# Seven products of quarters for eight in part of the last matrix product

## The chip, the core and the metric

The kernel runs on one core of a Trainium2 chip. The metric is the device time of one execution in microseconds (us). Three runs of the kernel before took 991.89 to 992.03 us, with a median of 991.94. Engines are named as in the profile: PE is TensorE (matmuls; PEld is its loading of stationary operands), DVE is VectorE, ACT is ScalarE, POOL is GpSimd and SP is SyncE, which here only issues the loads.

## The reference

The reference is a decoder trunk of two layers over 256 tokens of 1024 channels in float32. Each layer is a half-weighted gated feed-forward step, an attention step, and a second feed-forward step; at the end there is an RMS norm. The change lies in the last feed-forward step and the last norm:

```python
def swiglu(h, w_gate, w_up, w_down):
    return (jax.nn.silu(h @ w_gate) * (h @ w_up)) @ w_down
...
        h = h + FFN_RESIDUAL_WEIGHT * swiglu(rmsnorm(h, ffn2_norm[layer]),
                                             ffn2_w_gate[layer], ffn2_w_up[layer], ffn2_w_down[layer])
...
    return rmsnorm(h, final_norm)
```

The inner width of the feed-forward step is 2816, that is 22 blocks of 128. The last product is therefore (256 x 2816) times (2816 x 1024).

## The kernel before, in words

**Numbers in two parts.** Each float32 operand x is kept as a high part in the matmul's rounded float32 format (written by ACT as a copy) and a low part (written by DVE as x minus the high part). A product of two such operands is three matmuls: high by high, high by low, low by high (`product`, L179 to L186, where the three lines L182, L184 and L186 are these three). Weights come from memory as raw tiles of 1 MB, 4 of which fit (`rawp`), and are split into pieces of 1024 columns, high parts (`wh`) by ACT and low parts (`wl`) by DVE, for each of which there are 8 slots (`wp`). Four raw tiles and eight pieces are two units of gate and up weights each.

**Up to the last step** the residual stream `hT` is kept with channels on partitions. Four gate/up stages, three down products and two attention mixers run one after the other, each fed in the same way.

**The gate/up stage** (`ffn_blocks`, L340) of the last step goes over 11 pairs of blocks f, f + 1. For each pair SP loads 1 MB of gate and 1 MB of up weights. For each block TensorE does 8 matmuls of 512 columns for gate, 8 for up (L193), then 8 of 256 each for the low weights (L196). `close` turns the two accumulators into the block: ACT copies one half (L336), DVE adds the other (L337), multiplies the gate by the norm's row (L352), ACT applies SiLU (L353), POOL multiplies the up half by the row (L355), DVE multiplies both (L356), and ACT and DVE split the result (L94, L90). The block is held as 128 inner channels by 256 tokens, high and low, until the last product has used it.

**Turning the stream** (L688 to L694): between the gate/up stage and the last product, TensorE transposes `hT` in 16 pieces of 128 x 128 into four PSUM tiles (L693), and ACT copies them to `h`, now with tokens on partitions: two token tiles t of 128 rows, two column halves c of 512.

**The last product** (`down_last`, L408): the blocks are the stationary operand and the weights the moving one. It has four accumulators, one for each (t, c). For each of the first 18 blocks there are 12 matmuls of 512 columns: 2 t, 2 c, 3 matmuls each. The last four blocks are held back, so that the four accumulators end one after the other; each is then added to `h` by DVE (L432, L439), squared and summed (L711, L707), multiplied by the gains (L715), and after each token tile scaled by the reciprocal root (L728, L729) and stored. Of the last quarter the second half goes to an accumulator of its own, so that the last of this work is small.

**What sets the order.** Every engine works through its own instruction list in order. The lists come from the program's order of calls and a scheduler that moves an instruction ahead where its inputs allow it; tiles are handed out in rotation, and who gets a tile waits for the last reader of the one before.

Of the kernel before, what the change touches and what calls it, by code (L numbers as in the profile page):

```python
# [25 lines left out]
NG = H // HG  # L26
ROT = 16
HALF = ROT // 2
LEAD = 4
EPS = 1e-6  # L30
SCALE = DH ** -0.5
# [31 lines left out]
def trunk(ctx: ExitStack, tc: tile.TileContext, a: dict, out: bass.AP):  # L63
    nc = tc.nc
    PS = bass.MemoryType.PSUM
    const = ctx.enter_context(tc.tile_pool(name="const", bufs=1))
    rawp = ctx.enter_context(tc.tile_pool(name="rawp", bufs=4))
    wp = ctx.enter_context(tc.tile_pool(name="wp", bufs=8))
    xp = ctx.enter_context(tc.tile_pool(name="xp", bufs=1))
# [7 lines left out]
    def atile(shape, dt=F32, name="a"):  # L77
        return ap_.tile(shape, dt, tag="a", name=name)

    def acc(name):  # L80
        return accp.tile([P, 512], F32, tag="acc", name=name)

    def flat(ap):
        return ap.rearrange("p c n -> p (c n)")

    def parts_of(hi, lo, src, scale=1.0, later=None):

        def rest():
            if isinstance(scale, float):
                nc.vector.tensor_sub(lo, src, hi.bitcast(F32))  # L90
# [3 lines left out]
        nc.scalar.activation(hi, src, AF.Copy, scale=scale)  # L94
        (later or (lambda call: call()))(rest)
# [80 lines left out]
    def rows(w, k0, k, c0, n):  # L176
        return w[k0 * P:(k0 + k) * P, c0:c0 + n].rearrange("(k p) n -> p k n", p=P)

    def product(accs, xh, xl, ws, first, last):  # L179

        for ac, (wh, wl) in zip(accs, ws):
            nc.tensor.matmul(ac, xh, wh, start=first, stop=False)  # L182
        for ac, (wh, wl) in zip(accs, ws):
            nc.tensor.matmul(ac, xh, wl, start=False, stop=False)  # L184
        for ac, (wh, wl) in zip(accs, ws):
            nc.tensor.matmul(ac, xl, wh, start=False, stop=last)  # L186
# [94 lines left out]
    class Pieces:  # L281
# [55 lines left out]
        nc.vector.tensor_add(s, ac[:, :S], s)  # L337
        return s

    def ffn_blocks(name, wg, wu, norm, first=None, beside=()):  # L340

        blocks = []

        def both(f, pair):
            acs = [acc(f"{name}_{n}{f}") for n in "gu"]
            cols = slice(f % 2 * P, (f % 2 + 1) * P)
            products_t(acs, [[(wh[:, cols], wl[:, cols]) for wh, wl in w] for w in pair], norm.x, True, True)
            return acs

        def close(f, gate, up):  # L350
            g = joined(gate, f"{name}_g{f}")
            nc.vector.tensor_mul(g, g, norm.row)  # L352
            nc.scalar.activation(g, g, AF.Silu)  # L353
            u = joined(up, f"{name}_u{f}")
            nc.gpsimd.tensor_tensor(u, u, norm.row, op=ALU.mult)  # L355
            nc.vector.tensor_mul(g, g, u)  # L356
# [48 lines left out]
        down_t(name, wd, blocks, after)  # L405


    def down_last(name, w, nk, blocks, h, weight, part, after, tail=4):  # L408


        accs = [[acc(f"dn_{name}_{t}_{c}") for c in range(2)] for t in range(NT)]
        held = []

        def cut(ws, cols):
            return tuple(w[:, cols] for w in ws)

        halves = [slice(c * 512, (c + 1) * 512) for c in range(2)]
        for u in range(nk // 2):
            for i, ws in enumerate(unit(f"{name}_{u}", 2, D, [(None, rows(w, 2 * u, 2, 0, D))])):
                k = 2 * u + i  # L420
                if k < nk - tail:
                    for t in range(NT):
                        product(accs[t], *blocks[t][k], [cut(ws, half) for half in halves], k == 0, False)
                else:
                    held.append((k, ws))
        for t in range(NT):
            for c, half in enumerate(halves):
                n = 512 if (t, c) != (1, 1) else S
                for k, ws in held:
                    product([accs[t][c][:, :n]], *blocks[t][k], [cut(ws, slice(half.start, half.start + n))], False,  # L430
                            k == nk - 1)
                nc.vector.scalar_tensor_tensor(h[t][c], accs[t][c], weight, h[t][c], op0=ALU.mult, op1=ALU.add)  # L432
                part(t, slice(half.start, half.start + n))
            if t:
                end = acc(f"dn_{name}_end")[:, :S]
                for k, ws in held:
                    product([end], *blocks[t][k], [cut(ws, slice(D - S, D))], k == nk - tail, k == nk - 1)
                hc = h[1][1][:, S:]
                nc.vector.scalar_tensor_tensor(hc, end, weight, hc, op0=ALU.mult, op1=ALU.add)  # L439
                part(t, slice(D - S, D), True)  # L440
            after(t)

    def out_t(name, pieces, base, blocks, norm, tail=3):
# [242 lines left out]
    blocks = ffn_blocks("f21", a["ffn2_w_gate"][1], a["ffn2_w_up"][1], n6)  # L686

    h = [[xp.tile([P, 512], F32, tag=f"kx{2 * t + c}", name=f"h_{t}_{c}") for c in range(2)] for t in range(NT)]  # L688
    for t in range(NT):
        for c in range(2):  # L690
            tr = trt(f"h_{t}_{c}")
            for k in range(4):
                nc.tensor.transpose(tr[:, k * P:(k + 1) * P], hT[:, 4 * c + k, t * P:(t + 1) * P], ident)  # L693
            nc.scalar.activation(h[t][c], tr, AF.Copy)  # L694

    parts = [[], []]
    outs = [[None, None] for t in range(NT)]
# [26 lines left out]
    def finish(t):  # L724
# [8 lines left out]
    down_last("f21_d", a["ffn2_w_down"][1], KF,  # L733
              [[tuple(x[:, i, t * P:(t + 1) * P] for i in range(2)) for x in blocks] for t in range(NT)],
              h, 0.5, finish_part, finish)


_INS = ["ffn1_w_gate", "ffn1_w_up", "ffn1_w_down", "ffn2_w_gate", "ffn2_w_up", "ffn2_w_down",
# [23 lines left out]
```

## Time and profile before

| | us |
|---|---|
| median of the three runs | 991.94 |
| the profiled execution | 992.04 |
| its span, first to last instruction | 990.2 |
| last gate/up pair (f = 20, 21) on TensorE | 11.13 (911.20 to 922.33) |
| the 16 transposes | 1.82 (922.33 to 924.15) |
| first 18 blocks of the last product | 49.07 (923.90 to 972.97) |
| held blocks | 11.19 (972.97 to 984.16) |
| rest, to the end of the span | 6.0 |

Times inside the span are counted from its start. Matmuls overlap: one of 512 columns is shown with about 0.39 us, and the next starts after 0.23. A row of the timeline gives the start, the length, the engine, the line, the operation with the tiles it writes and reads, a count where several are merged, and in brackets how long the engine was idle before it and who ended that.

### The profile page before, as it was taken

The numbers are of one execution on the slowest core, as the hardware profiler recorded it, in microseconds if no ns is written. First come the engines' busy times: TensorE is split into PE (matmuls) and PEld (weight loads), VectorE is DVE, ScalarE is ACT, GpSimd is POOL, SyncE is SP. The second block draws the span as 40 slices with busy tenths as digits, with TensorE's granted clock in tenths as the row PEclk, the third lists the DMA queues.
The fourth block names the chain that finished last, engine by engine and source line by source line (L and its number), as shares of the span: only waits on it lengthen the run. The fifth ranks groups of instructions, "written<-read, shape, count | busy, mean of one in ns | idle before, by whom it ended". The sixth has DMA issues, their size and how long they took to land. (4 is left out here: it accounts for less than half of the span.)

```text
span 990.2 us, 15709 instructions
## 1 busy us (share of the span) xinstructions
PE 978.1 (99%) x5892; PEld 863.5 (87%) x5892; DVE 731.2 (74%) x1283; ACT 588.6 (59%) x1079; POOL 164.4 (17%) x194
## 2 busy tenths in 40 slices
PE   8999999999999999999999999999999999999997
PEld 5888888888899888888888888888889998888886
DVE  6987866667787788776678877666687878788642
ACT  7656654467776656655456566545677656665531
POOL 3211111122302211111121111111222022111000
PEclk9999999999999999999999999999999999999999
DMA  9776465653434565555645664666533345655611
GB/s 300 252 253 210 162 213 181 212 173 139 156 121 141 166 197 191 196 193 182 201 161 187 197 204 158 203 201 213 170 129 128 119 142 175 205 175 202 205 57 43
DMA packets 158573, 176.06 MB, mean 178 GB/s; under 512 B 3616, under 2 KB 152608, under 8 KB 158496
## 3 DMA queue, kind: packets, MB, share of 16 engines
q1 hardware_dynamic: 157776, 174.24, 53.6%
q8 instruction: 46, 0.75, 0.3%
q10 hardware_dynamic: 720, 0.82, 0.2%
q14 instruction: 31, 0.25, 0.1%
HBM read 173.99 MB, written 1.05 MB: 177 GB/s over the span
## 5 line engine op out<-in xcount | busy, mean ns | idle before, releaser
L193 PE MATMUL f_g<-x_n,wh_f_g 128*128 128x512 f32 x688 | 180.1, 394 | 0.0
L193 PE MATMUL f_u<-x_n,wh_f_u 128*128 128x512 f32 x688 | 177.3, 390 | 0.0
L193 PEld LDWEIGHTS f_u<-x_n,wh_f_u 128*128 128x128 f32 x688 | 129.1, 188 | 27.3
L193 PEld LDWEIGHTS f_g<-x_n,wh_f_g 128*128 128x128 f32 x688 | 124.1, 189 | 22.6
L355 POOL TENSOR_TENSOR j_f_u<-j_f_u,r_n 128x256 f32<-128x256 f32 x88 | 76.6, 872 | 378.9 <-DVE j_f_u L337 356.6
L193 PE MATMUL dn_f<-act_f,wh_f 128*128 128x512 f32 x528 | 126.5, 391 | 0.0
L157 DVE TENSOR_TENSOR wl_f_u<-raw_f_u,wh_f_u 128x1024 fp32r<-128x1024 f32 x86 | 120.4, 1401 | 1.8 <-ACT wh_f_u L156 1.7
L157 DVE TENSOR_TENSOR wl_f_g<-raw_f_g,wh_f_g 128x1024 fp32r<-128x1024 f32 x86 | 103.5, 1234 | 16.7 <-PE f_g L196 10.6
L193 PEld LDWEIGHTS dn_f<-act_f,wh_f 128*128 128x128 f32 x528 | 96.9, 188 | 18.6
L157 DVE TENSOR_TENSOR wl_f<-raw_f,wh_f 128x1024 fp32r<-128x1024 f32 x72 | 81.9, 1154 | 35.8 <-ACT wh_f L156 26.7
L196 PE MATMUL f_u<-x_n,wl_f_u 128*128 128x256 f32 x688 | 103.3, 283 | 0.0
L196 PE MATMUL f_g<-x_n,wl_f_g 128*128 128x256 f32 x688 | 102.9, 282 | 0.0
L196 PEld LDWEIGHTS f_g<-x_n,wl_f_g 128*128 128x128 f32 x688 | 96.5, 190 | 6.3
L156 ACT ACTIVATE wh_f_g<-raw_f_g 128x1024 fp32r<-128x1024 f32 x86 | 89.4, 1049 | 13.3 <-issue 6.0
L156 ACT ACTIVATE wh_f<-raw_f 128x1024 fp32r<-128x1024 f32 x72 | 67.3, 978 | 49.5 <-PE dn_f L193 27.2
L156 ACT ACTIVATE wh_f_u<-raw_f_u 128x1024 fp32r<-128x1024 f32 x86 | 86.6, 1046 | 15.2 <-PE f_g L193 10.9
L196 PEld LDWEIGHTS f_u<-x_n,wl_f_u 128*128 128x128 f32 x688 | 91.6, 192 | 0.0
L230 POOL TENSOR_TENSOR ss_n<-ss_n,sq_n 128x256 f32<-128x256 f32 x42 | 42.2, 1005 | 248.7 <-ACT sq_n L229 247.8
L94 ACT ACTIVATE act_f<-j_f_g 128x256 fp32r<-128x256 f32 x88 | 36.5, 417 | 72.0 <-DVE j_f_g L356 71.8
L353 ACT ACTIVATE j_f_g<-j_f_g 128x256 f32<-128x256 f32 x88 | 36.8, 418 | 66.6 <-DVE j_f_g L352 66.2
L196 PEld LDWEIGHTS dn_f<-act_f,wl_f 128*128 128x128 f32 x528 | 68.1, 191 | 2.8
L196 PE MATMUL dn_f<-act_f,wl_f 128*128 128x256 f32 x528 | 69.0, 283 | 0.0
(220 smaller groups left out, 1790.6 us busy)
## 6 DMA issues: line engine op xcount, KB each, us to landing
raw_f_g<-in_ffn_w_gate_dram SPq DMA_DIRECT2D x43, 1024.0 KB, 5.2
raw_f_u<-in_ffn_w_up_dram SPq DMA_DIRECT2D x43, 1024.0 KB, 5.2
raw_f<-in_ffn_w_down_dram SPq DMA_DIRECT2D x24, 1024.0 KB, 5.2
raw_f_d<-in_ffn_w_down_dram SPq DMA_DIRECT2D x11, 1024.0 KB, 4.8
raw_f<-in_ffn_w_down_dram SPq DMA_DIRECT2D x12, 768.0 KB, 4.6
raw_qka<-in_a_w_qkv_dram SPq DMA_DIRECT2D x16, 512.0 KB, 4.4
raw_kvb<-in_kv_w_dram SPq DMA_DIRECT2D x12, 512.0 KB, 4.2
raw_va<-in_a_w_qkv_dram SPq DMA_DIRECT2D x4, 1024.0 KB, 5.0
```

The costliest lines, as they stand in the source:

```text
L94: nc.scalar.activation(hi, src, AF.Copy, scale=scale)
L156: nc.scalar.activation(wh, r, AF.Copy)
L157: nc.vector.tensor_sub(wl, r, wh.bitcast(F32))
L193: nc.tensor.matmul(ac, wh, flat(x), start=first and i == 0, stop=False)
L196: nc.tensor.matmul(ac[:, :S], wl, x[:, 0, :], start=False, stop=last and i == len(ws) - 1)
L230: nc.gpsimd.tensor_tensor(self.ss, self.ss, sq, op=ALU.add)
L353: nc.scalar.activation(g, g, AF.Silu)
L355: nc.gpsimd.tensor_tensor(u, u, norm.row, op=ALU.mult)
```

## The change

A pair of blocks times its two rows of weight blocks is a 2 x 2 by 2 x 2 product of quarters: left quarters are (token tile t, block k), right quarters (block k, column half c). For the pairs `FAST` = 2, 3, 5, 6, 8 of eleven, the eight products of quarters become seven by Winograd's form. It needs four sums of left quarters, four sums of right quarters, and a final combination of the accumulators.

- **Left sums** (`quarter_sums`): when block 2i + 1 of a fast pair is closed, DVE makes the four sums `q` of 128 x 128 from the products of gate and up, which are kept in a tile `act2` of the pair; ACT and DVE split them into high and low, 512 columns. DVE's part of the split is issued after the split of the next block.
- **Right sums** (`load`): a fast pair's raw tile is a 2 x 2 of quarters of 512 columns. DVE makes two sums in one operation of 1024 columns, POOL makes the other two one after the other (the fourth reads the third), into a second raw tile. Seven quarters are split in four pieces: a (two quarters), b (one), c and d (two sums each).
- **Products** (`fast`): seven products of three matmuls, one accumulator each, in the order m1 and 11 (piece a), 12 (b), m5 and m7 (c), m6 and 21 (d). The accumulators are eight: the four quarters, m1, m5, m6 and m7; three of them are in the PSUM pool of the transposes.
- **Ordinary pairs** are split into two pieces per pair, as before, but a product goes to one accumulator at a time. The next pair is loaded and split before the products of a pair are issued.
- **Collection** (`collect`): after pair 8 and before the final sums, ACT, DVE and POOL put the combinations of m1, m5, m6 and m7 into `h`. The held blocks are 18 to 21, as before, and their end is as before.
- **Turning the stream** is now done inside the gate/up stage: a quarter of it ahead of each of the pairs f = 4, 6, 8, 10.

The core of the diff:

```diff
+FAST = (2, 3, 5, 6, 8)
...
+    def quarter_sums(x, hi, lo, name):
+        q = atile([P, 4, P], name=f"q_{name}")
+        x = x.rearrange("p a (t n) -> p (a t) n", n=P)
+        nc.vector.tensor_sub(q[:, :2], x[:, 0::3], x[:, 1:2].to_broadcast([P, 2, P]))
+        nc.vector.tensor_add(q[:, 2], q[:, 1], x[:, 0])
+        nc.vector.tensor_sub(q[:, 3], x[:, 2], q[:, 2])
+        rest = []
+        parts_of(hi, lo, flat(q), later=rest.append)
+        return rest
...
-            nc.vector.tensor_mul(g, g, u)
+            pair = f // 2
+            if sums is not None and pair in sums:
+                if f % 2 == 0:
+                    pairs[pair] = atile([P, 2, S], name=f"act2_{name}_{f}")
+                prod = pairs[pair][:, f % 2]
+            else:
+                prod = g
+            nc.vector.tensor_mul(prod, g, u)
             x = atile([P, 2, S], F32R, name=f"act_{name}_{f}")
-            parts_of(x[:, 0], x[:, 1], g)
+            parts_of(x[:, 0], x[:, 1], prod)
+            while rest:
+                rest.pop(0)()
+            if prod is not g and f % 2:
+                rest.extend(quarter_sums(pairs.pop(pair), *sums[pair], f"{name}_{f}"))
             blocks.append(x)
...
+        c11, c12, c21, m1, m5 = [acc(f"dn_{name}_{n}") for n in ("11", "12", "21", "m1", "m5")]
+        c22, m6, m7 = [trt(f"dn_{name}_{n}") for n in ("22", "m6", "m7")]
...
+        def load(i):
+            raw = rawp.tile([P, 4, 512], F32, tag="raw", name=f"raw_{name}_{i}")
+            nc.sync.dma_start(raw.rearrange("p (k c) n -> p k (c n)", k=2), rows(w, 2 * i, 2, 0, D))
+            if i not in sums:
+                return split(raw[:, :2], f"{i}a") + split(raw[:, 2:], f"{i}b")
+            t = rawp.tile([P, 4, 512], F32, tag="raw", name=f"sum_{name}_{i}")
+            nc.vector.tensor_add(t[:, :2], raw[:, 0::3], raw[:, 1:2].to_broadcast([P, 2, 512]))
+            nc.gpsimd.tensor_tensor(t[:, 2], t[:, 0], raw[:, 3], op=ALU.add)
+            nc.gpsimd.tensor_tensor(t[:, 3], t[:, 2], raw[:, 2], op=ALU.add)
+            b11, b21 = split(raw[:, 0::2], f"{i}a")
+            b22, = split(raw[:, 3:], f"{i}b")
+            ta, tc = split(t[:, :2], f"{i}c")
+            tb, td = split(t[:, 2:], f"{i}d")
+            return b11, b21, b22, ta, tc, tb, td
...
+            for n, ac, left, right in (("1", m1, x[0][0], b11), ("11", c11, x[0][1], b21), ("12", c12, l3, b22),
+                                       ("5", m5, l5, ta), ("7", m7, l7, tc), ("6", m6, l6, tb),
+                                       ("21", c21, x[1][1], td)):
+                add(n, ac, left, right, last and len(n) == 1)
...
+        def collect():
+            a, b, c, d = [atile([P, 512], name=f"co_{name}_{n}") for n in "abcd"]
+            nc.scalar.activation(a, m1, AF.Copy, scale=weight)
+            nc.vector.scalar_tensor_tensor(b, m6, weight, a, op0=ALU.mult, op1=ALU.subtract)
+            nc.gpsimd.tensor_tensor(h[0][0], h[0][0], a, op=ALU.add)
+            nc.vector.scalar_tensor_tensor(c, m7, weight, b, op0=ALU.mult, op1=ALU.subtract)
+            nc.vector.scalar_tensor_tensor(b, m5, -weight, b, op0=ALU.mult, op1=ALU.add)
+            nc.gpsimd.tensor_tensor(h[0][1], h[0][1], b, op=ALU.add)
+            nc.vector.scalar_tensor_tensor(d, m5, -weight, c, op0=ALU.mult, op1=ALU.subtract)
+            nc.vector.tensor_add(h[1][0], h[1][0], c)
+            nc.vector.tensor_add(h[1][1], h[1][1], d)
...
+        for i in range(pairs):
+            if i + 1 < pairs:
+                ahead.append(load(i + 1))
+            ws = ahead.pop(0)
+            if i in sums:
+                fast(i, ws)
...
+    turns = [lambda t=t, c=c: turn_h(t, c) for t in range(NT) for c in range(2)]
+    blocks = ffn_blocks("f21", a["ffn2_w_gate"][1], a["ffn2_w_up"][1], n6, beside=[lambda: None] + turns, sums=sums)
```

More of the change, by code (lines that the diff above doesn't have):

```diff
@@ L338, in joined, with ffn_blocks @@
         return s
-    def ffn_blocks(name, wg, wu, norm, first=None, beside=()):
-        blocks = []
+    def quarter_sums(x, hi, lo, name):
[7 more added lines that the diff above has]
+        return rest
+    def ffn_blocks(name, wg, wu, norm, first=None, beside=(), sums=None):
+        blocks, pairs, rest = [], {}, []
         def both(f, pair):
@@ L405, in ffn, with down_last, add, split @@
         down_t(name, wd, blocks, after)
[L408 to L421, printed above, removed]
-                    for t in range(NT):
-                        product(accs[t], *blocks[t][k], [cut(ws, half) for half in halves], k == 0, False)
-                else:
-                    held.append((k, ws))
+    def down_last(name, w, blocks, sums, h, weight, part, after, tail=2):
+        c11, c12, c21, m1, m5 = [acc(f"dn_{name}_{n}") for n in ("11", "12", "21", "m1", "m5")]
+        c22, m6, m7 = [trt(f"dn_{name}_{n}") for n in ("22", "m6", "m7")]
+        begun = set()
+        def add(n, ac, x, ws, last=False):
+            product([ac], *x, [ws], n not in begun, last)
+            begun.add(n)
+        def split(src, n):
+            wh, wl = [wp.tile([P, src.shape[1], 512], F32R, tag=tag, name=f"{tag}_{name}_{n}") for tag in ("wh", "wl")]
+            nc.scalar.activation(wh, src, AF.Copy)
+            nc.vector.tensor_sub(wl, src, wh.bitcast(F32))
+            return [(wh[:, i, :], wl[:, i, :]) for i in range(src.shape[1])]
+        def load(i):
[12 more added lines that the diff above has]
+            return b11, b21, b22, ta, tc, tb, td
+        def fast(i, ws):
+            b11, b21, b22, ta, tc, tb, td = ws
+            l7, l5, l6, l3 = [tuple(v[:, j * P:(j + 1) * P] for v in sums[i]) for j in range(4)]
+            x = [[blocks[t][2 * i + k] for k in range(2)] for t in range(NT)]
+            last = i == max(sums)
+            for n, ac, left, right in (("1", m1, x[0][0], b11), ("11", c11, x[0][1], b21), ("12", c12, l3, b22),
[13 more added lines that the diff above has]
+            nc.vector.tensor_add(h[1][1], h[1][1], d)
+        quarters = [[("11", c11), ("12", c12)], [("21", c21), ("22", c22)]]
+        pairs = KF // 2
+        ahead, held = [load(0)], []
+        for i in range(pairs):
[4 more added lines that the diff above has]
+                fast(i, ws)
+            elif i < pairs - tail:
+                for k in range(2):
+                    for t in range(NT):
+                        for c in range(2):
+                            add(*quarters[t][c], blocks[t][2 * i + k], ws[2 * k + c])
+            else:
+                held += [(2 * i + k, ws[2 * k:2 * k + 2]) for k in range(2)]
+        collect()
+        end = acc(f"dn_{name}_end")[:, :S]
@@ L426, in down_last @@
         for t in range(NT):
-            for c, half in enumerate(halves):
-                n = 512 if (t, c) != (1, 1) else S
+            for c in range(2):
+                n, ac = quarters[t][c]
+                cut = 512 if (t, c) != (1, 1) else S
                 for k, ws in held:
[L430 to L433, printed above, removed]
+                    add(n, ac[:, :cut], blocks[t][k], tuple(v[:, :cut] for v in ws[c]), k == KF - 1)
+                nc.vector.scalar_tensor_tensor(h[t][c], ac, weight, h[t][c], op0=ALU.mult, op1=ALU.add)
+                part(t, slice(c * 512, c * 512 + cut))
@@ L434, in down_last @@
             if t:
-                end = acc(f"dn_{name}_end")[:, :S]
                 for k, ws in held:
-                    product([end], *blocks[t][k], [cut(ws, slice(D - S, D))], k == nk - tail, k == nk - 1)
+                    add("end", end, blocks[t][k], tuple(v[:, S:] for v in ws[1]), k == KF - 1)
                 hc = h[1][1][:, S:]
                 nc.vector.scalar_tensor_tensor(hc, end, weight, hc, op0=ALU.mult, op1=ALU.add)
-                part(t, slice(D - S, D), True)
+                part(t, slice(512 + S, 1024), True)
@@ L685, in trunk, with turn_h @@
     mixer("b", segs_b, a["b_w_o"][0], masks[:, 1, :], n6)
-    blocks = ffn_blocks("f21", a["ffn2_w_gate"][1], a["ffn2_w_up"][1], n6)
-    h = [[xp.tile([P, 512], F32, tag=f"kx{2 * t + c}", name=f"h_{t}_{c}") for c in range(2)] for t in range(NT)]
[L689 to L694, printed above, removed]
+    sums = {}
+    for n, i in enumerate(FAST):
+        if n < 4:
+            parts = ap_.tile([P, 2, 512], F32R, tag=("qkh", "qkl")[n % 2], name=f"left_{i}", bufs=2)
+            sums[i] = (parts[:, 0], parts[:, 1])
+        else:
+            sums[i] = tuple(xp.tile([P, 512], F32R, tag=f"kx{4 + 2 * (n - 4) + j}", name=f"left_{i}_{j}") for j in range(2))
+    h = [[xp.tile([P, 512], F32, tag=f"kx{2 * t + c}", name=f"h_{t}_{c}") for c in range(2)] for t in range(NT)]
+    def turn_h(t, c):
+        tr = trt(f"h_{t}_{c}")
+        for k in range(4):
+            nc.tensor.transpose(tr[:, k * P:(k + 1) * P], hT[:, 4 * c + k, t * P:(t + 1) * P], ident)
+        nc.scalar.activation(h[t][c], tr, AF.Copy)
+    turns = [lambda t=t, c=c: turn_h(t, c) for t in range(NT) for c in range(2)]
+    blocks = ffn_blocks("f21", a["ffn2_w_gate"][1], a["ffn2_w_up"][1], n6, beside=[lambda: None] + turns, sums=sums)
     parts = [[], []]
@@ L731, in finish @@
             (nc.scalar, nc.sync)[c].dma_start(out[0, t * P:(t + 1) * P, c * 512:(c + 1) * 512], outs[t][c])
-    down_last("f21_d", a["ffn2_w_down"][1], KF,
+    down_last("f21_d", a["ffn2_w_down"][1],
               [[tuple(x[:, i, t * P:(t + 1) * P] for i in range(2)) for x in blocks] for t in range(NT)],
-              h, 0.5, finish_part, finish)
+              sums, h, 0.5, finish_part, finish)
 _INS = ["ffn1_w_gate", "ffn1_w_up", "ffn1_w_down", "ffn2_w_gate", "ffn2_w_up", "ffn2_w_down",
```

## The prediction

> **What bounds the kernel now.** I read the page's busy shares first, then the stage at the end of the span by stretches, then the chain of waits, then single instructions there.
>
> ```profile
> PE 978.1 (99%) x5892; PEld 863.5 (87%) x5892; DVE 731.2 (74%) x1283; ACT 588.6 (59%) x1079; POOL 164.4 (17%) x194
> 911.20:922.33 11.13, 11.13 (x66) 9.83 (x66) 8.79 (x15) 6.77 (x14) 1.54 (x2) 1.00 0.55 190
> 922.33:924.15 1.82, 1.82 (x17) 1.73 (x16) 1.82 (x4) 1.82 (x6) 0.05 (x1) 1.00 0.00 0
> 923.90:972.97 49.07, 49.07 (x219) 40.65 (x218) 21.04 (x20) 16.57 (x19) 0.79 (x1) 1.00 0.32 108
> 972.97:984.16 11.19, 11.19 (x61) 9.58 (x59) 5.57 (x9) 3.41 (x9) 0.88 (x2) 1.00 0.13 48
> ```
>
> TensorE is busy 99% of the span, and in the four stretches (columns: length, then busy time and count of PE, PEld, DVE, ACT, POOL, then granted clock, DMA share, GB/s) it never stops: last gate/up pair, turning of the residual stream, first 18 blocks of the last product, its four held blocks. The clock is 1.00 throughout. In the last product DVE has 21.04 of 49.07 us to do, ACT 16.57, POOL 0.79. The chain agrees: until the last matmul it is TensorE alone.
>
> ```profile
> 922.33 1.82 PE h L693 x16
> 924.15 0.47 PE dn_f_d L182 x2
> ...
> 978.12 0.23 PE dn_f_d L184
> 978.35 0.24 PE dn_f_d L186
> 978.59 0.02 issue
> 978.61 0.70 DVE h L432
> ```
>
> So a matmul taken out there is worth its slot, as long as every weight piece is ready in time. The slot: 216 matmuls (18 blocks x 12) lie in the 49.07 us of the third stretch, 0.227 us each; held matmuls, which go one accumulator at a time as all new ones do, have the same.
>
> ```profile
> 972.97 0.39 PE L182 MATMUL dn_f_d<-wh_f_d,act_f 128*128 128x512 f32 x1
> ...
> 980.91 0.39 PE L186 MATMUL dn_f_d<-wh_f_d,act_f 128*128 128x512 f32 x1
> ```
>
> These are the first and last of 36: 7.94 us over 35 steps is 0.227.
>
> **The change, part by part.**
>
> *Removed.* A pair of blocks is 8 quarter products of 3 matmuls; in pairs 2, 3, 5, 6 and 8 it becomes 7. The two programs' instruction lists for TensorE differ by 15 matmuls of 512 columns. 15 x 0.227 = **-3.40 us** while TensorE is fed. An ordinary pair then lasts 5.45 us, a fast one 4.76. I call the start of the product T = 0: pair 2 begins at T 10.9, 3 at 15.7, 4 at 20.4, 5 at 25.9, 6 at 30.6, 7 at 35.4, 8 at 40.9, the held blocks at 45.6.
>
> The rows for the next two parts, in this order: DVE operations of 512 and 128 columns, DVE's idle stretches in one gate/up period, DVE's first pieces of the last product, and TensorE's first use of the pieces written at 898.66:
>
> ```profile
> 982.28 0.69 DVE L715 TENSOR_TENSOR out<-h,gfin 128x512 f32<-128x512 f32 x1
> L246 DVE TENSOR_SCALAR diag_n<-ident,c_n 128x128 f32<-128x128 f32 x2 | 0.5, 284 | 0.8 <-POOL c_n L239 0.8
> 896.43 0.43 DVE L356 TENSOR_TENSOR j_f_g<-j_f_g,j_f_u 128x256 f32<-128x256 f32 x1 [0.92 <-POOL j_f_u L355]
> 897.34 0.43 DVE L90 TENSOR_TENSOR act_f<-j_f_g,act_f 128x256 fp32r<-128x256 f32 x1 [0.48 <-ACT act_f L94]
> 898.66 2.36 DVE L157 TENSOR_TENSOR wl_f_g<-raw_f_g,wh_f_g 128x1024 fp32r<-128x1024 f32 x2 [0.90 <-PE f_g L196]
> 909.79 2.36 DVE L157 TENSOR_TENSOR wl_f_d<-raw_f_d,wh_f_d 128x1024 fp32r<-128x1024 f32 x2 [0.90 <-PE f_g L196]
> 914.80 1.00 PE L196 MATMUL f_g<-x_n,wl_f_g 128*128 128x256 f32 x7
> ```
>
> *Moved: the 16 transposes.* They take 1.82 us of TensorE in a row before, and four times 0.46 ahead of the gate/up pairs f = 4, 6, 8, 10 after: net 0. They cover nothing that would now be late: the first weight pieces of the product are written from 909.79 on, 14 us ahead of 923.90. ACT's four copies (L694) move with them to where it is busy 6.77 of 11.13 us.
>
> *Added in the gate/up stage.* For each fast pair DVE gets the sums of quarters and ACT and DVE the split of 512 columns; the in-place product of gate and up only gets another target.
>
> DVE's addition is one operation of 256 columns (0.43), two of 128 (between 0.28, a 128-column operation with one tensor input, and 0.43) and one of 512 (0.69): 1.7 to 2.0 us for each of five periods of 11.13 us, in which DVE idles 0.92 + 0.48 + 0.90 = 2.30 us. The last of these is a wait for a weight slot, and the piece written at 898.66 to 901.02 is first read at 914.80: 13.8 us of lead behind that. All five additions, 10 us at most and with no idle time used, fit into the lead. **0 us**, between 0 and 0.5.
>
> *Added in the last product.* Of a fast pair's raw tile DVE makes two sums (1024 columns), POOL two more (512 each, in a row), and four pieces a, b, c, d (1024, 512, 1024, 1024) are split for two of 1024. What one costs:
>
> ```profile
> L230 POOL TENSOR_TENSOR ss_n<-ss_n,sq_n x42: 730/1002/1597, 8.8 to 803.7; 128x256 f32<-128x256 f32 x42
> 857.55 0.79 POOL L355 TENSOR_TENSOR j_f_u<-j_f_u,r_n 128x256 f32<-128x256 f32 x1 [4.96 <-DVE j_f_u L337]
> 857.66 1.77 DVE L157 TENSOR_TENSOR wl_f_u<-raw_f_u,wh_f_u 128x1024 fp32r<-128x1024 f32 x1
> L156 ACT ACTIVATE wh_f_d<-raw_f_d 128x1024 fp32r<-128x1024 f32 x15 | 15.9, 1060 | 21.7 <-PE dn_f_d L186 21.7
> raw_f_d<-in_ffn_w_down_dram SPq DMA_DIRECT2D x11, 1024.0 KB, 4.8
> ```
>
> DVE: 1.18 per 1024 columns (2.36 for two, above), so 4.5 x 1.18 = 5.3 us for a fast pair, 2.36 for an ordinary one; ACT 3.5 x 1.06 = 3.7. A POOL add of 512 columns isn't in the trace: twice the shortest and the longest of 256 (ns: shortest/median/longest in the L230 row) gives 1.5 to 3.2, and I take twice the median, 2.0, as its partner is this busy DVE. Beside a POOL operation of 0.79 the 1024-column DVE one takes 1.77 for 1.18: DVE loses 0.59, three quarters of POOL's time.
>
> The balance: from about T 5 (behind the last gate/up product DVE still has four closing operations of 0.42 and the pieces 2b, 2c, 2d of 0.6, 1.18 and 1.18, 4.6 us) to T 47.6 (when the last held piece is read) DVE has pairs 3, 5, 6, 8 at 5.3 and 4, 7, 9, 10 at 2.36: 30.7 of 42.6 us, a reserve of 11.9. The six POOL adds of pairs 5, 6, 8 take 6 x 2.0 x 0.75 = 9.0 of it. It fits.
>
> Then the waits, in DVE's order. The pieces have 8 slots, the raw tiles 4, of which a fast pair now takes two. Pair 3's pieces wait for those of pairs 0 and 1: slots free at T 2.7, 5.4, 8.2, 10.9. In front of 3c DVE's queue has the sum of pair 5, whose load SP can issue only when the sum tile of pair 2 is free (about T 5) and which lands 4.8 us later: T 10. Behind it 3c and 3d (each up to 1.77) end by about T 13 and 15; TensorE reads 3c at 15.7 + 9 x 0.227 = 17.7 and 3d at 19.1. That is the tightest place: **4 us of reserve**. Pairs 5, 6 and 8 come out 5 to 7 us early in the same way, since each slot is freed a pair and a half before it is read. POOL's sums of pairs 2 and 3 stand in front of POOL's products of blocks 19 and 21; DVE's closing of pairs 9 and 10 waits for these, and TensorE reads those blocks from T 45.6 on only. SP issues the same 11 loads. **0 us**, between 0 and the rival below.
>
> *Added at the end: the collection.* One ACT copy, six DVE operations of 512 columns and two POOL adds go in front of DVE's first final sum.
>
> ```profile
> 975.89 0.69 DVE L432 SCALAR_TENSOR_TENSOR h<-dn_f_d,h 128x512 f32<-128x512 f32 x1 [11.28 <-PE dn_f_d L186]
> 976.62 0.69 DVE L715 TENSOR_TENSOR out<-h,gfin 128x512 f32<-128x512 f32 x1
> 978.61 0.69 DVE L432 SCALAR_TENSOR_TENSOR h<-dn_f_d,h 128x512 f32<-128x512 f32 x1 [1.30 <-PE dn_f_d L186]
> 979.34 0.69 DVE L715 TENSOR_TENSOR out<-h,gfin 128x512 f32<-128x512 f32 x1
> 984.20 0.42 DVE L439 SCALAR_TENSOR_TENSOR h<-dn_f_d_end,h 128x256 f32<-128x256 f32 x1 [0.17 <-PE dn_f_d_end L186]
> ```
>
> In the clock of before: the product that the collection needs last ends 15 matmuls ahead of the first final sum, at 975.89 - 3.40 = 972.49. Six operations of 0.61 to 0.73 put it to about 976.5; the first final sum and its product with the gains then end at 978.0, and the second sum, due at 978.61, is on time. POOL's second add runs beside the last of these and may stretch them by 0.75 x 2.0 = 1.5: 0.9 late there; how much of that is left at the last sum, which has an idle 0.17 us before it, depends on what idles between. I take **+0.1**, between 0 and 0.8.
>
> **Sum.** -3.40 + 0.1 = -3.3 us. The profiled execution took 992.04 us (span 990.2 and 1.84 around it, unchanged), 0.10 over the median of 991.94: 988.74 by its clock, **988.6** by the median.
>
> **The rivals.** What a measurement of this kernel can tell from no change is about 0.2%, 2 us: faster means under 989.96, slower above 993.92.
>
> *A, slower: DVE and POOL block each other and DVE becomes the bound of the last product.* For it: the row of 1.77, and POOL adds of 256 up to 1.597. Price: adds of 3.2 us, all lost to DVE, are 6 x 3.2 = 19.2 against a reserve of 11.9: TensorE waits 7.3 us, 988.6 + 7.3 = 996. It decides from 11.9 / 6 = 2.0 us lost per add; the gain is gone at 2.5. Against it: DVE lost 0.75 of POOL's time, and a blocked POOL waits instead, which costs only its own lead. The Trainium skill, "SBUF — State Buffer", section "Who interferes with whom", says that a VectorE instruction with two SBUF inputs contends with a GpSimd one that reads SBUF, and calls the shared port pair an exclusive lock. The rows above agree in kind, with 0.59 lost beside 0.79; with all of POOL's time lost the sum would be 6 x 2.0 = 12.0, at the edge. Chance 0.11.
>
> *B, a partial stall.* Slots and raw tiles come back late at one place (the load for pair 5, or the second of two fast pairs in a row), more than the 4 us of reserve by 1 to 3 us: 989.6 to 991.6. For it: a fast pair holds half the raw tiles, and its piece d needs five steps in a row (DVE 1.18, POOL 2.0, 2.0, ACT 1.06, DVE 1.18, 7.4 us) while TensorE spends 4.76. Against it: these steps lie one pair and more ahead. Chance 0.13.
>
> *C, the collection makes the last sums late* by the full 0.8: 989.3. Chance 0.04.
>
> That the change doesn't take the matmuls out is excluded by the instruction lists.
>
> **How the numbers follow.** The forecast, 988.2 to 989.0, has 0.72. Faster: forecast, C and 0.05 of B, 0.81; same: the rest of B, 0.08; slower: A, 0.11. The range 988.2 to 990.3 holds the forecast, C and the lower part of B, about 0.8.
>
> **What would show it.** Right: 15 matmul slots fewer in the last product, 0.227 us each, no idle TensorE between T 0 and the end, the last matmul 3.4 us earlier; DVE waiting for ACT or TensorE, not TensorE for DVE, in pairs 3 to 8; gate/up still 11.13 us a pair. Wrong: TensorE idle in front of a matmul of piece c or d, released by DVE; POOL adds over 2.5 us with DVE pieces of 2 us beside them; the first final sum later than the second's due time.

## The result, and the profile after

| | before | after |
|---|---|---|
| median (us) | 991.80 (8 runs, 990.94 to 992.26) | 994.81 (8 runs, 994.54 to 995.31) |
| profiled execution, its span (us) | 992.04, 990.2 | 994.54, 992.8 |
| start of the last product, T = 0 (us) | 923.90 | 923.36 |
| start of the last matmul / of the last sum into h (us) | 983.88 / 984.20 | 984.37 / 986.68 |

The changed kernel takes 1.0032 of the time of before (95% interval 1.0023 to 1.0040): 3.0 us slower, where I forecast 3.3 faster and held the whole range below 990.3. The forecast was wrong; of its cases rival A, at 0.11, lies nearest.

First the page's busy shares of after, then its stretches (columns as before: length, then busy time and count of PE, PEld, DVE, ACT, POOL, then granted clock, DMA share, GB/s).

```profile
PE 976.5 (98%) x5877; PEld 860.4 (87%) x5877; DVE 761.6 (77%) x1324; ACT 597.1 (60%) x1095; POOL 192.8 (19%) x206
```

```profile
913.00:924.20 11.20, 11.20 (x66) 9.91 (x65) 10.53 (x16) 5.55 (x12) 3.83 (x3) 1.00 0.27 94
924.20:940.00 15.80, 15.80 (x72) 13.06 (x71) 10.83 (x15) 10.30 (x16) 4.98 (x4) 1.00 0.39 134
940.00:945.00 5.00, 4.12 (x17) 2.78 (x16) 5.00 (x4) 1.87 (x3) 4.14 (x2) 1.00 0.05 5
945.00:950.00 5.00, 4.45 (x19) 3.30 (x18) 5.00 (x5) 1.83 (x2) 0.07 (x1) 1.00 0.63 206
950.00:970.00 20.00, 19.92 (x88) 16.18 (x87) 16.31 (x15) 9.77 (x12) 8.85 (x4) 1.00 0.59 211
970.00:975.00 5.00, 4.33 (x19) 3.00 (x17) 5.00 (x4) 2.92 (x4) 1.46 (x1) 1.00 0.00 0
975.00:980.00 5.00, 4.41 (x19) 3.68 (x20) 4.93 (x7) 0.00 (x0) 1.29 (x1) 1.00 0.00 0
```

TensorE has the 15 matmuls fewer, and its clock is still 1.00. The gate/up stage and the first 16 us of the product run without a gap. Then come four stretches of 5 us in which PE is busy 4.12 to 4.45 us and DVE all the time or nearly: 74 matmuls lie there, where 88 slots of 0.227 us have room. The waits of PE from 920 us on name whom it waits for (columns: sum, times, longest, in us):

```profile
PE dn_f_d L185 <- DVE wl_f_d_10b L450: 1.3, 1, 1.3
PE dn_f_d_m L185 <- DVE wl_f_d_3d L450: 0.6, 1, 0.6
PE dn_f_d L185 <- DVE wl_f_d_4a L450: 0.6, 1, 0.6
PE dn_f_d_m L185 <- DVE wl_f_d_3c L450: 0.3, 1, 0.3
```

TensorE waits for DVE, as the prediction's last part listed under "wrong". The chain of waits, which was TensorE alone up to the last matmul, has TensorE no longer in its shares by engine:

```profile
DVE 3%; POOL 1%; issue 1%; ACT 1%; DMA 1%; POOLq 0%; ACTq 0%; SPq 0%
```

DVE's instructions one by one (start, duration, line; in brackets the idle time before it and who ended it):

```profile
932.90 1.22 DVE L450 TENSOR_TENSOR wl_f_d_2d<-sum_f_d,wh_f_d_2d 128x1024 fp32r<-128x1024 f32 x1
...
939.34 1.23 DVE L459 TENSOR_TENSOR sum_f_d<-raw_f_d 128x1024 f32<-128x1024 f32 x1 [3.15 <-DMA raw_f_d<-in_ffn_w_down_dram]
940.48 1.22 DVE L450 TENSOR_TENSOR wl_f_d_3c<-sum_f_d,wh_f_d_3c 128x1024 fp32r<-128x1024 f32 x1
941.61 2.31 DVE L450 TENSOR_TENSOR wl_f_d_3d<-sum_f_d,wh_f_d_3d 128x1024 fp32r<-128x1024 f32 x1
943.85 2.30 DVE L450 TENSOR_TENSOR wl_f_d_4a<-raw_f_d,wh_f_d_4a 128x1024 fp32r<-128x1024 f32 x1
...
954.09 1.21 DVE L450 TENSOR_TENSOR wl_f_d_6c<-sum_f_d,wh_f_d_6c 128x1024 fp32r<-128x1024 f32 x1
958.94 1.22 DVE L450 TENSOR_TENSOR wl_f_d_6d<-sum_f_d,wh_f_d_6d 128x1024 fp32r<-128x1024 f32 x1 [3.64 <-ACT wh_f_d_6d L449]
960.09 1.22 DVE L450 TENSOR_TENSOR wl_f_d_7a<-raw_f_d,wh_f_d_7a 128x1024 fp32r<-128x1024 f32 x1
...
964.63 1.77 DVE L450 TENSOR_TENSOR wl_f_d_8b<-raw_f_d,wh_f_d_8b 128x512 fp32r<-128x512 f32 x1
966.33 2.31 DVE L450 TENSOR_TENSOR wl_f_d_8c<-sum_f_d,wh_f_d_8c 128x1024 fp32r<-128x1024 f32 x1
...
973.24 2.31 DVE L450 TENSOR_TENSOR wl_f_d_10b<-raw_f_d,wh_f_d_10b 128x1024 fp32r<-128x1024 f32 x1
975.46 0.68 DVE L482 SCALAR_TENSOR_TENSOR co_f_d_b<-dn_f_d_m,co_f_d_a 128x512 f32<-128x512 f32 x1
...
977.51 0.68 DVE L487 SCALAR_TENSOR_TENSOR co_f_d_d<-dn_f_d_m,co_f_d_c 128x512 f32<-128x512 f32 x1
978.11 1.40 DVE L488 TENSOR_TENSOR h<-h,co_f_d_c 128x512 f32<-128x512 f32 x1
...
980.03 0.68 DVE L515 SCALAR_TENSOR_TENSOR h<-dn_f_d,h 128x512 f32<-128x512 f32 x1
...
986.68 0.42 DVE L521 SCALAR_TENSOR_TENSOR h<-dn_f_d_end,h 128x256 f32<-128x256 f32 x1
```

And POOL's beside them:

```profile
940.78 2.06 POOL L460 TENSOR_TENSOR sum_f_d<-sum_f_d,raw_f_d 128x512 f32<-128x512 f32 x1 [8.26 <-DVE sum_f_d L459]
942.92 2.15 POOL L461 TENSOR_TENSOR sum_f_d<-sum_f_d,raw_f_d 128x512 f32<-128x512 f32 x1
952.56 3.89 POOL L460 TENSOR_TENSOR sum_f_d<-sum_f_d,raw_f_d 128x512 f32<-128x512 f32 x1 [7.50 <-DVE sum_f_d L459]
956.53 1.29 POOL L461 TENSOR_TENSOR sum_f_d<-sum_f_d,raw_f_d 128x512 f32<-128x512 f32 x1
963.80 2.05 POOL L460 TENSOR_TENSOR sum_f_d<-sum_f_d,raw_f_d 128x512 f32<-128x512 f32 x1 [5.99 <-DVE sum_f_d L459]
...
973.00 1.46 POOL L483 TENSOR_TENSOR h<-h,co_f_d_a 128x512 f32<-128x512 f32 x1 [5.44 <-ACT co_f_d_a L481]
977.67 1.29 POOL L486 TENSOR_TENSOR h<-h,co_f_d_b 128x512 f32<-128x512 f32 x1 [3.21 <-DVE co_f_d_b L485]
```

Read the two side by side. POOL's add of 940.78 ends at 942.84; the piece 3d, started at 941.61, takes 2.31 us instead of 1.21, and ends at 943.92, 1.08 us behind that add. POOL's next add, started at 942.92, ends 1.15 behind 3d; 4a ends 1.08 behind this one. They go by turns. At 952.56 POOL's add lasts through three DVE operations in a row (the last, 6c, ends at 955.30) and ends at 956.45, 1.15 later.

From these rows comes the account of DVE's time. 2d ends near T 10.7 (934.03, when the next operation starts, less 923.36), and 10b, the last piece, at T 52.2. Of the 41.5 us between, DVE waits 3.15 for the load of pair 5 and 3.64 for 6d, and is held 5.5 in five pieces (3d, 4a, 8b, 8c, 10b: each 1.1 over its usual time), which leaves 29.2 of work. TensorE could use 10b from T 47.6 on: 4.6 us late.

TensorE's part of the loss: from the first to the last matmul 61.01 us, before 59.98; 59.98 - 3.40 = 56.58, so 4.4 us of stalls. (The list of waits above has only 2.8 of them: it counts from the shown end of a matmul, some 0.4 us behind its start, where the next could start after 0.23.) The last sum into h starts 2.31 us behind the start of the last matmul, before 0.32: 2.0 more. -3.40 + 4.43 + 1.99 = +3.02, counted from T = 0. The two medians differ by 3.01, the two profiled executions only by 2.50: in the one of after the product starts 0.54 us earlier, a start that moves between 922.69 and 924.04 over the profiled executions of this document.

### The profile page after: what moved, and what is told of

It is laid out like the page before. It is cut to its first block, busy times and chain, and to the rows that moved or that the text cites. A ratio compares the mean times of both kernels' runs of the same rounds, so it can differ in the third digit from the quotient of the medians.

```text
span 992.8 us, 15762 instructions
## 1 busy us (share of the span) xinstructions
PE 976.5 (98%) x5877; PEld 860.4 (87%) x5877; DVE 761.6 (77%) x1324; ACT 597.1 (60%) x1095; POOL 192.8 (19%) x206
## 5 line engine op out<-in xcount | busy, mean ns | idle before, releaser
L370 POOL TENSOR_TENSOR j_f_u<-j_f_u,r_n 128x256 f32<-128x256 f32 x88 | 83.9, 955 | 374.4 <-DVE j_f_u L338 352.0
L95 ACT ACTIVATE act_f<-j_f_g 128x256 fp32r<-128x256 f32 x78 | 32.3, 417 | 65.9 <-DVE j_f_g L378 65.7
```

## The experiments

Theory L: POOL's adds and DVE's two-input operations hold each other up, and DVE, already late from the sums, becomes the bound of the last product and of the collection. Rivals: the moved transposes or the new order cost the time; it is a chain of waits (DVE's sum, POOL's two, ACT, DVE for piece d) and not a lack of DVE time; it is the collection; it is one early tight place. In the expectations B is the backlog that DVE brings along from the left sums (not the prediction's rival B), K is the collection, and M is the moved transposes or the new order in e1 and the early tight place in e10. All edits are of the changed kernel. Ratios are to the kernel before, run anew beside each group (medians 991.76 beside e1 to e4, 991.83 beside e5 to e8, 991.72 beside e9 and e10), with 95% intervals. "Last sum" is its start after T = 0, each kernel by its own product start; before it is T 60.30, after T 63.32.

| run | median (us) | ratio | 10b ends | last sum |
|---|---|---|---|---|
| e1_no_fast | 991.87 | 0.9999 [0.9990, 1.0009] | T 40.6 | T 60.21 |
| e2_no_right_sums | 988.36 | 0.9965 [0.9952, 0.9978] | T 43.4 | T 56.82 |
| e3_no_left_sums | 993.12 | 1.0015 [1.0005, 1.0024] | T 50.5 | T 61.64 |
| e4_sums_on_dve | 988.52 | 0.9967 [0.9954, 0.9980] | T 45.7 | T 56.81 |
| e5_adds_unread | 994.03 | 1.0018 [1.0009, 1.0027] | T 51.2 | T 62.31 |
| e6_spread_pairs | 989.73 | 0.9979 [0.9970, 0.9988] | T 44.7 | T 58.18 |
| e7_all_on_dve | 988.30 | 0.9965 [0.9951, 0.9979] | T 44.5 | T 56.82 |
| e8_six_pairs | 988.23 | 0.9961 [0.9946, 0.9976] | T 45.2 | T 56.85 |
| e9_coll_on_dve | 994.15 | 1.0026 [1.0017, 1.0036] | T 51.0 | T 62.64 |
| e10_late_sums_on_dve | 990.62 | 0.9989 [0.9980, 0.9998] | T 47.8 | T 58.99 |

Read the last two columns together. After the change 10b ends at T 52.2; there, and in e3, e4, e5 and e10, the last sum starts 11.1 to 11.2 us behind the end of 10b, and 11.6 in e8 and e9, where DVE makes two additions more. In these runs DVE has only one idle stretch of more than 0.2 us between the two (1.13 us, for POOL's rms). So in them the end follows the moment at which DVE is done with 10b, however long TensorE stalled on the way.

**e1: no fast pair**, the rest of the change stays (transposes amid the gate/up stage, new order of the product).

```diff
-FAST = (2, 3, 5, 6, 8)
+FAST = ()
```

> The changed kernel with no fast pair: the transposes amid the gate/up stage, one accumulator at a time, loads a pair ahead, but eight products everywhere and no collection. Theory B (DVE's backlog from the left sums) and theory L (DVE and POOL block each other over the right sums) both expect the time of before, 991.8 +- 0.5. A third, M (the moved transposes or the new order of products cost something themselves), expects 993 or more.

991.87: the time of before. So the moved transposes and the new order cost nothing, and the loss comes from the fast pairs alone.

**e2: no right sums.**

```diff
-            t = rawp.tile([P, 4, 512], F32, tag="raw", name=f"sum_{name}_{i}")
-            nc.vector.tensor_add(t[:, :2], raw[:, 0::3], raw[:, 1:2].to_broadcast([P, 2, 512]))
-            nc.gpsimd.tensor_tensor(t[:, 2], t[:, 0], raw[:, 3], op=ALU.add)
-            nc.gpsimd.tensor_tensor(t[:, 3], t[:, 2], raw[:, 2], op=ALU.add)
+            t = raw
```

> Leaves out the sums of right quarters: the pieces c and d are split from the raw tile, no second raw tile, no DVE and POOL adds; everything else stays, the left sums too. L: the stalls before matmuls of pairs 3, 4, 6 and of the held blocks (4.4 us in all) go, 988.5 to 990. B: the gate/up stage hands over the same backlog of DVE, at least the stalls at pairs 3 and 4 stay, 991 to 993.

988.36, and no wait of TensorE is left: the fewer matmuls bring their 3.4 us (last sum T 56.82, where 60.30 - 3.40 = 56.90). The whole loss hangs on making the right sums: without them the left sums, which are still made, cost nothing either. The collection, on POOL still, costs nothing here. The time lies just under L's range.

**e3: no left sums.**

```diff
-            l7, l5, l6, l3 = [tuple(v[:, j * P:(j + 1) * P] for v in sums[i]) for j in range(4)]
+            l7, l5, l6, l3 = x[0] + x[1]
...
-    blocks = ffn_blocks("f21", a["ffn2_w_gate"][1], a["ffn2_w_up"][1], n6, beside=[lambda: None] + turns, sums=sums)
+    blocks = ffn_blocks("f21", a["ffn2_w_gate"][1], a["ffn2_w_up"][1], n6, beside=[lambda: None] + turns)
```

> Leaves out the sums of left quarters: fast products take the blocks themselves as left operands; the right sums stay. B: DVE enters the last product about 5 us earlier, no stall at pairs 3 and 4, 989 to 990.5. L: POOL's sums still hold up ACT and DVE at pairs 6 and 8, 992.5 to 994.5.

993.12, inside L's range and not B's: 1.7 us less than the changed kernel. 2d starts at T 7.85 instead of 9.54, and everything behind it comes that much earlier. The left sums make no gap in the gate/up stage, but their cost is carried on into the product. So B is a part of the loss, but DVE comes 1.7 us earlier and not the 5 that B asked for.

**e4: POOL's two right sums on DVE.**

```diff
-            nc.gpsimd.tensor_tensor(t[:, 2], t[:, 0], raw[:, 3], op=ALU.add)
-            nc.gpsimd.tensor_tensor(t[:, 3], t[:, 2], raw[:, 2], op=ALU.add)
+            nc.vector.tensor_tensor(t[:, 2], t[:, 0], raw[:, 3], op=ALU.add)
+            nc.vector.tensor_tensor(t[:, 3], t[:, 2], raw[:, 2], op=ALU.add)
```

> The two right sums of POOL are made by DVE instead (two operations of 512 columns, 0.6 us each, per fast pair). L: no blocking and no step on POOL in the chain, 989 to 991. B: DVE has 6 us more to do in all, the stalls at pairs 3 and 4 grow, 994.5 to 997.

988.52, faster than both kernels and 0.5 under L's range, with no wait of TensorE listed. The same computation, with more instructions on the busy engine and fewer on the idle one, is 6.3 us shorter. Its DVE timeline:

```profile
937.44 1.22 DVE L459 TENSOR_TENSOR sum_f_d<-raw_f_d 128x1024 f32<-128x1024 f32 x1 [3.31 <-DMA raw_f_d<-in_ffn_w_down_dram]
938.58 1.22 DVE L450 TENSOR_TENSOR wl_f_d_3c<-sum_f_d,wh_f_d_3c 128x1024 fp32r<-128x1024 f32 x1
...
940.32 1.22 DVE L450 TENSOR_TENSOR wl_f_d_3d<-sum_f_d,wh_f_d_3d 128x1024 fp32r<-128x1024 f32 x1
942.05 1.22 DVE L450 TENSOR_TENSOR wl_f_d_4a<-raw_f_d,wh_f_d_4a 128x1024 fp32r<-128x1024 f32 x1
...
967.03 2.31 DVE L450 TENSOR_TENSOR wl_f_d_10b<-raw_f_d,wh_f_d_10b 128x1024 fp32r<-128x1024 f32 x1
969.27 0.68 DVE L482 SCALAR_TENSOR_TENSOR co_f_d_b<-dn_f_d_m,co_f_d_a 128x512 f32<-128x512 f32 x1
```

The wait for the load of pair 5 is as long as in the changed kernel, though it ends 2.2 us earlier (T 13.8), and 3d and 4a take 1.22. Only 10b and the collection's L488 (1.41) are still held, each beside one of POOL's additions to h. A row from this run's group of the sums gives the price on DVE (ns, shortest/median/longest), beside the same line of the changed kernel on POOL:

```profile
L460 DVE TENSOR_TENSOR sum_f_d<-sum_f_d,raw_f_d x5: 680/682/685, 912.9 to 959.4; 128x512 f32<-128x512 f32 x5
```

```profile
L460 POOL TENSOR_TENSOR sum_f_d<-sum_f_d,raw_f_d x5: 1277/2051/3887, 911.5 to 963.8; 128x512 f32<-128x512 f32 x5
```

**e5: POOL makes the same adds into tiles that nobody reads;** piece d is split from the raw tile.

```diff
-            nc.gpsimd.tensor_tensor(t[:, 2], t[:, 0], raw[:, 3], op=ALU.add)
-            nc.gpsimd.tensor_tensor(t[:, 3], t[:, 2], raw[:, 2], op=ALU.add)
+            scrap = [xp.tile([P, 512], F32, tag=f"kx{6 + j}", name=f"scrap_{i}_{j}") for j in range(2)]
+            nc.gpsimd.tensor_tensor(scrap[0], t[:, 0], raw[:, 3], op=ALU.add)
+            nc.gpsimd.tensor_tensor(scrap[1], scrap[0], raw[:, 2], op=ALU.add)
...
-            tb, td = split(t[:, 2:], f"{i}d")
+            tb, td = split(raw[:, 2:], f"{i}d")
```

> POOL makes the same two adds per fast pair, with the same inputs, but into a scrap tile that nobody reads; the piece d is split from the raw tile instead, so the last two sums are left out of the product. POOL still runs beside DVE, but no engine waits for its sums. If the blocking beside each other alone makes the loss: 992 to 994.5. If the loss is the chain, ACT and DVE standing in order behind POOL's sums: 988.3 to 989.5.

994.03: 5.5 of the 6.3 us that lie between the changed kernel and e4 remain although no piece waits for a POOL sum. The chain of waits is rejected as the main cause. It is no exact copy of the changed kernel: the wait for 6d is gone, but seven pieces are held instead of five (7.7 us), and the sum of pair 5 starts at T 17.7, 1.7 us later. The pieces 4a and 4b show the held durations:

```profile
943.84 2.32 DVE L450 TENSOR_TENSOR wl_f_d_4a<-raw_f_d,wh_f_d_4a 128x1024 fp32r<-128x1024 f32 x1
946.09 2.31 DVE L450 TENSOR_TENSOR wl_f_d_4b<-raw_f_d,wh_f_d_4b 128x1024 fp32r<-128x1024 f32 x1
```

**e6: three fast pairs, spread,** sums on POOL.

```diff
-FAST = (2, 3, 5, 6, 8)
+FAST = (2, 5, 8)
```

> The changed kernel with three fast pairs, none next to another (2, 5, 8), nine matmuls fewer, 2.04 us. If the loss is one of saturation (a fast pair's chain needs more than its 4.76 us but an ordinary pair between makes up for it): 989.7 to 990.7. If every fast pair costs more than it saves: 3/5 of the loss, 993 to 994.

989.73: nine matmuls fewer at 0.227 are 2.04 us, and 991.83 (before, in the same runs) - 2.04 = 989.8. Three pairs lose nothing, though their pieces are held just as long; DVE has idle time left that takes it in:

```profile
949.90 2.32 DVE L450 TENSOR_TENSOR wl_f_d_7a<-raw_f_d,wh_f_d_7a 128x1024 fp32r<-128x1024 f32 x1
952.14 2.31 DVE L450 TENSOR_TENSOR wl_f_d_7b<-raw_f_d,wh_f_d_7b 128x1024 fp32r<-128x1024 f32 x1
...
964.32 1.23 DVE L450 TENSOR_TENSOR wl_f_d_10a<-raw_f_d,wh_f_d_10a 128x1024 fp32r<-128x1024 f32 x1 [1.50 <-ACT wh_f_d_10a L449]
```

So it is a bound that is reached, not a price per fast pair.

**e7: as e4, and the collection's two additions on DVE too. e8: as e7, with pair 1 fast as well.**

```diff
-            nc.gpsimd.tensor_tensor(h[0][0], h[0][0], a, op=ALU.add)
+            nc.vector.tensor_add(h[0][0], h[0][0], a)
...
-            nc.gpsimd.tensor_tensor(h[0][1], h[0][1], b, op=ALU.add)
+            nc.vector.tensor_add(h[0][1], h[0][1], b)
```

```diff
-FAST = (2, 3, 5, 6, 8)
+FAST = (1, 2, 3, 5, 6, 8)
```

> As with the right sums on DVE, and the two POOL adds of the collection on DVE too. Blocking: the last weight piece takes 1.2 us instead of 2.3 and the adds of h 0.7 instead of 1.4, against 1.2 us more on DVE: within 0.4 us of 988.5. If the collection on DVE makes the final sums late: 989.5 or more.

> All sums on DVE and six fast pairs (1, 2, 3, 5, 6, 8), three matmuls fewer again, 0.68 us. If DVE without POOL beside it has time left: 987.5 to 988.1. If DVE is now the bound: 988.5 to 991, with TensorE waiting for its pieces.

988.30 and 988.23: no difference from e4 that can be told; e8 lies between its two expected ranges. With six pairs the last matmul starts at T 55.82 instead of 56.50, 0.7 earlier, but the last sum at T 56.85 as in e7 (56.82). In e7 it still waits 0.16 us for TensorE, in e8 for nobody:

```profile
979.90 0.42 DVE L521 SCALAR_TENSOR_TENSOR h<-dn_f_d_end,h 128x256 f32<-128x256 f32 x1 [0.16 <-PE dn_f_d_end L187]
```

```profile
979.54 0.42 DVE L521 SCALAR_TENSOR_TENSOR h<-dn_f_d_end,h 128x256 f32<-128x256 f32 x1
```

The sixth pair's gain is given back at the end: there DVE is the bound even without POOL.

**e9: only the collection's two additions on DVE** (the first edit of e7), the right sums stay on POOL.

> The changed kernel with one edit: the collection's two additions to h go from POOL to DVE; the ten sums of right quarters stay on POOL. Theory L (a DVE operation beside a POOL one is held for as long as that one runs, and DVE, late from the right sums, is the bound): piece 10b falls from 2.31 to 1.22, TensorE's wait for it from 1.3 to about 0.2, and the stretched 1.40 of the collection to 0.68; against that DVE gets two operations of 0.69. Balance at the first final sum: -1.09 - 0.72 + 1.38 = -0.4, so about 994.4, and the span still ends some 2 us later behind TensorE's end than before, since DVE is late all the same. Rival K (the late end is made by the two POOL additions of the collection): the 2.1 us behind TensorE's end and the 1.3 at 10b go, 991.4.

994.15, 0.7 below the changed kernel: theory L's 994.4 nearly, and not K's 991.4. 10b takes 1.22, the wait for it falls from 1.3 to 0.2, but the last sum is only 0.7 earlier: DVE is late at the end because it comes late to the collection.

**e10: POOL keeps the right sums of pairs 2 and 3 only.**

```diff
-            nc.gpsimd.tensor_tensor(t[:, 2], t[:, 0], raw[:, 3], op=ALU.add)
+            (nc.gpsimd if i < 4 else nc.vector).tensor_tensor(t[:, 2], t[:, 0], raw[:, 3], op=ALU.add)
```

(and the same for the second sum)

> The changed kernel with one edit: the two POOL sums of pairs 5, 6 and 8 go to DVE, those of pairs 2 and 3 (made beside the gate/up stage) stay on POOL, and so do the collection's. Theory L (held operations use up DVE's reserve in the last product): the load for pair 5 and its sum still come as late as in the changed kernel (939.3), TensorE still waits up to 0.5 us in front of 3c to 4a, but the later waits go and the end is as in the version with all sums on DVE: 988.6 to 989.4. Rival M (the place that decides is the early backlog alone: late 2d, late load, 3c and 3d; once late, DVE never comes back): 991.5 to 994.8.

990.62: between L's 988.6 to 989.4 and M's 991.5 to 994.8, so neither number came. It divides the loss: POOL's adds of pairs 5, 6 and 8 cost 994.81 - 990.62 = 4.2 us, those of pairs 2 and 3, beside the gate/up stage, 990.62 - 988.52 = 2.1 (in this order; the other was not run, and the parts need not be the same in it). L's mechanism holds for the larger part. My number for it missed that DVE has no idle time by which it could make up the late start: the first piece of the collection runs in the queue directly behind 10b, and the last sum is 2.2 us later than in e4, as 10b's end is. TensorE's last matmul is 1.3 us later than in e4 (T 57.81 and 56.50), nearly all of it lost in front of 3c to 4a; its listed waits are 0.3.

```profile
969.39 2.31 DVE L450 TENSOR_TENSOR wl_f_d_10b<-raw_f_d,wh_f_d_10b 128x1024 fp32r<-128x1024 f32 x1
971.63 0.68 DVE L482 SCALAR_TENSOR_TENSOR co_f_d_b<-dn_f_d_m,co_f_d_a 128x512 f32<-128x512 f32 x1
...
982.85 0.42 DVE L521 SCALAR_TENSOR_TENSOR h<-dn_f_d_end,h 128x256 f32<-128x256 f32 x1
```

## Why the prediction was wrong, step by step

- **Removed, -3.40: right.** In e2 and e4 the last sum comes 3.48 and 3.49 us earlier after T = 0 than before.
- **Moved transposes, 0: right** (e1).
- **Left sums, 0, between 0 and 0.5: wrong by 1.7** (e3). TensorE's lead of 13.8 us did cover them, so that the gate/up stage has no gap. But a lead used up isn't given back: DVE entered the next stage late, and there the time was missing. I had closed the account at the stage's end.
- **Right sums, 0: the step that failed.** In detail:
  - "From about T 5 ... a reserve of 11.9" was the mis-sized term. Behind T 5 the balance counted DVE's work and POOL's interference, but it started 5.7 us too early (2d was done at T 10.7, not 5) and left out DVE's own waits. Of the late start, measured by when 2d starts, 1.7 us are the left sums (e3), and 2.4 come from POOL instead of DVE making the right sums of pairs 2 and 3 (T 9.54 after, 7.14 in e4). With no right sums at all 2d starts at T 5.73 (e2), so making these sums puts 3.8 us on it.
  - "3c and 3d ... 4 us of reserve": the load for pair 5 does wait for 2d, as the step said; so 2d's delay passed whole to the sum of pair 5, which started at T 16.0 behind a wait of 3.15 instead of at T 10, and the reserve was gone at the place that I had called the tightest.
  - The price of POOL's six adds, "9.0", was about right: 4.4 us in four held pieces and 3.64 of waiting for 6d, whose add was held in its turn, make 8.0. What was wrong with it is that I subtracted it from 11.9. From T 10.7 to T 47.6 there are 36.9 us, and DVE needed 41.5: 4.6 too many, and TensorE stalled 4.4. As one sum: of the forecast's 11.9 - 9.0 = 2.9 the late start takes 5.7, the wait for the load 3.15 and the hold of 10b by the collection's add 1.1; POOL's adds give back 1.0 and DVE's work 1.5 (29.2 for 30.7, most of it because pair 3's sum was already made).
- **Collection, +0.1: +2.0.** The step's own sum holds where DVE comes in time: in e4 the last sum is at T 56.81, in e2, where DVE waits 1.84 us for TensorE ahead of the collection, at 56.82. After the change DVE reached it at T 52.1 instead of T 45.2 (e2) or 45.6 (e4). The six operations in DVE's queue cost nothing until DVE is late; then every one of them lies on the path. e9 shows that POOL's two additions make only a small part of it.
- **The rivals.** A was right in its kind (DVE becomes the bound) and near in its time, 996 against 994.8, but not by its price: it asked for adds of 3.2 us, and the median is 2.05 and 1.37. It came true from the other end, because the reserve was smaller. "A blocked POOL waits instead, which costs only its own lead" was the argument against it: the one add that was held longest (3.89) made DVE itself wait 3.64 for 6d, by way of POOL's second add and ACT's copy. B's mechanism, the load for pair 5, happened as well, inside A. The chance of 0.11 was too low; the profile of before already showed the row of 1.77 and a POOL operation of 1.6, and a full hold by turns would have been the right reading: that DVE piece ends at 859.43, 1.09 behind the POOL operation's end at 858.34, just as 3d and 4a do here. All of POOL's time behind the start of the piece was lost, not three quarters of it.
- **The Trainium skill,** "SBUF — State Buffer", section "Who interferes with whom": its exclusive lock fits the rows better than my 0.75. A piece beside a POOL add ends 1.08 us behind it, as if it had only then begun.

What stays open: what the late load of pair 5 costs by itself. In e4 DVE waits 3.31 us for it and TensorE loses nothing; in e10, where its sum starts at T 15.9, as late as after the change, the stalls in front of 3c to 4a remain. No run gave the sum tiles a pool of their own, which should let SP issue that load earlier. And how the two engines take turns: at 952.56 POOL's add lets three DVE operations pass, elsewhere one.

## What to carry to other kernels

Moving a two-input add from a busy DVE to an idle POOL saved nothing here: 0.68 us of DVE per add against 1.1 in which a DVE operation is held, and the version with the adds on DVE is 6.3 us faster. When an engine gets work in a stage where it has a lead, follow the lead into the next stage: make the balance of the engine from the moment at which it is really free, with its waits in it, up to the moment at which its last result is needed. Then ask what lies in its queue behind that moment, for it will be late by the whole excess.

## What was not expected of the hardware

- A DVE operation with two inputs that meets a POOL add, where this one has gone first, waits for its end as a whole. The usual 1.21 to 1.22 us for 1024 columns becomes 2.30 to 2.32 in each of the cases shown (five kernels), and 512 columns take 1.77 for 0.68 (8b) or 1.40 (L488, which starts 0.44 behind the add). What is constant is the end: 1.08 to 1.09 us behind the add's for 1024 columns, 0.55 for 512 in both rows. So the extra is what is left of the add, and not a share of the operation's own rate.
- The hold goes both ways and isn't even: POOL's add of 512 columns takes 1.29 us while DVE is idle (956.53) and 2.06, 2.15 or 3.89 when it comes behind one, one or three DVE operations. An operation of the collection that reads one of its inputs from PSUM (L487, 977.51) doesn't hold it: the add of 977.67 beside it takes 1.29.
- DVE operations in one queue start 1.13 to 1.15 us apart where each lasts 1.22 (940.48 and 941.61, 958.94 and 960.09 above): durations of a queue that never idles add up to more than its time. From 2d to 10b they come, without what is held, to 31.2 us, and DVE spent 29.2.
